# Products of 64x64 quadrants in two shared PSUM banks, in the heads stage of an RWKV-7 layer

## The chip, the cores and the metric

The kernel runs on one core of a Trainium2 chip. The metric is the device time of one execution in microseconds (us); before the change it is 1110.01 us, the median of three runs (1109.58 to 1110.29). TensorE does the matrix products, VectorE and ScalarE (DVE and ACT in the rows) the element work, GpSimd (POOL) some of it, and SyncE (SP) starts the transfers. TensorE writes its results to PSUM, which has banks of 128 partitions by 512 fp32 values.

## What is computed

A trunk of two layers on a sequence of 256 tokens with 1024 features, all in fp32. Each layer has a half-step SwiGLU FFN, a mixer and a second half-step FFN, each behind an RMS norm. The first mixer is a short gated convolution, the second is RWKV-7 time mixing with 16 heads of size 64. The change lies in the second:

```python
def wkv7_scan(r, w, k, v, a, b):          # per head: S is 64 x 64, one step per token
    def step(S, inp):
        r_t, w_t, k_t, v_t, a_t, b_t = inp
        sa = jnp.einsum('bhij,bhj->bhi', S, a_t)
        S = S * w_t[:, :, None, :] + sa[..., None] * b_t[:, :, None, :] + v_t[..., None] * k_t[:, :, None, :]
        y = jnp.einsum('bhij,bhj->bhi', S, r_t)
        return S, y
...
    y = wkv7_scan(rh, decay, kh, vh, -kk, kk * ah)
    # y is then normalised per head, gets a bonus of (r . k) v, is multiplied by the gate g
    return (y * g) @ w_o, v_first
```

## The kernel before

**Stages.** The first FFN and the convolution layer come first, then the FFN of the second layer, the inputs of the RWKV layer, its heads stage (`rwkv_heads`, L841 to L1129; 706 to 932 us of the trace) and the final FFN. Weights are streamed from HBM throughout. Large products are made of three float32r products of high and low halves (L110 to L112); the small ones of the heads stage are plain fp32 products (`mm`, L54) and transposes (`tp`, L57).

**Blocks.** The scan is done in chunks of 64 tokens. A block n is one of four groups of four heads and one half of the sequence (128 tokens, two chunks c): eight blocks in all. On a tile of 128 partitions the two halves e of the rows belong to two heads, so that a 64x64 product of a head uses one quadrant of TensorE's array, or a whole-array product uses a block-diagonal weight. Each block has four parts:

- `front(n)`: the gates and decays (`z`, `sa`, `am`, `cum`), transposes of four factors (`wT`), the scores, and the copies `bkt` (token-major factors, L940 and L941). The scores are two groups of four products of 64 rows by 128 columns (L54, into `G` for e = 0 and into the bank `G1` for e = 1). From each group `copy_predicated` (L931) puts the strictly lower part into `xfix`, and two masked products make `ar` (L936) and `br` (L938).
- `inverse(n)`, in `wkv_inverse` (L498 to L552): the inverse of four unit triangular 64x64 matrices on each row half, by doubling: levels l = 1, 2, 4, 8, 16, 32. Each level transposes the last result (L516, VectorE), copies it (`xr`, L509 or L512, ScalarE), masks the transposed one (L519 at level 1, L522 after that, VectorE) and multiplies on TensorE into the bank `xr`. At levels 2 to 16 the masked weight `pd` is 128x512: for each of four matrices a block-diagonal 128x128 weight, so four whole-array products. At levels 1 and 32 there are eight 64x64 products. Level 32 has its weights `p` from two 32-row transposes (L529) and no mask.
- `chain(n)`, in `wkv_chunk`: for the two chunks the recurrence of the state, all in the bank `ch`.
- `finish(n)`: normalisation of `y`, the gate product `g` (L991, L992) and its use (L998), transposes `oT` of the result, and its split into `oh` (ScalarE, L115) and `ol` (VectorE, L116). `g` and `oT` lie in the bank `fin`.

Projections of r, k and v for later groups and the output products (`pj`) are cut into pieces that fill TensorE between these steps.

**Order.** It is written by hand: `scores` (L1074 to L1081) has strings of letters for the steps (I an inverse step, C chain, F front, N finish, * a filler). In cycle n chain(n), inverse(n+1), finish(n−1) and front(n+2) are interleaved. VectorE and ScalarE run in the program's order (`manual_schedule`), and TensorE's products are kept in it too. Waits between engines are put in by the framework for whatever overlaps; accesses of two engines to one PSUM bank are put one after the other.

**Banks.** Eight banks: `G`, `xr`, `ch`, `fin`, two `pj` and two that are shared by the transposes and by `z`, `cum`, `G1` (`tr`). The final FFN uses the first six again (L1106, L1128).

Of the kernel before, what the change touches and what calls it, by code (L numbers as in the profile page):

```python
# [25 lines left out]
class Trunk:  # L26
# [50 lines left out]
    def bank(self, tag, name=None):  # L77
        return self.ps.tile([128, 512], F32, tag=tag, name=name or tag, bufs=self.bank_bufs[tag])
# [345 lines left out]
    def wkv_constants(self):  # L424

        nc = self.nc
# [17 lines left out]
        for l in (1, 2, 4, 8, 16):  # L444
            self.lev[l] = m = self.fixed_cols(64 if l == 1 else 128)
            nc.gpsimd.memset(m, 0.0)
            for e in range(2):
                r = slice(64 * e, 64 * e + 64)
                me = m[r] if l == 1 else m[r, 64 * e:64 * e + 64]
# [43 lines left out]
    def wkv_inverse(self, pool, u, par):  # L493
# [5 lines left out]
        src = None  # L499

        def ready(l):

            old = x0 if l == 1 else src[:, :, 1]
            xr = pool.tile([128, 4, 2, 64], F32, name=f"xr{par}", bufs=1) if l > 1 else None

            def rest():
                if l > 2:
                    n = 2 if l < 32 else 1
                    nc.scalar.copy(xr[:, :, 0:n], src[:, :, 0:n])  # L509
                elif l == 2:  # L510
                    nc.gpsimd.tensor_tensor(xr[:, :, 0], x0, all4(self.lev1T), ALU.mult)
                    nc.scalar.copy(xr[:, :, 1], src[:, :, 1])  # L512

            if l < 32:
                pb = pool.tile([128, 4, 64], F32, name=f"pb{par}", bufs=1)
                nc.vector.transpose(pb, old)  # L516
                rest()
                if l == 1:
                    nc.vector.tensor_tensor(pb, pb, all4(self.lev[l]), ALU.mult)  # L519
                else:  # L520
                    pd = pool.tile([128, 4, 2, 64], F32, name=f"pd{par}", bufs=1)
                    nc.vector.tensor_tensor(pd, pb.unsqueeze(2).broadcast_to([128, 4, 2, 64]),  # L522
                                            self.lev[l].rearrange("p (e m) -> p e m", e=2).unsqueeze(1).broadcast_to([128, 4, 2, 64]), ALU.mult)
                    pb = pd
            else:
                pb = p32
                for e in range(2):
                    lo, hi = slice(64 * e, 64 * e + 32), slice(64 * e + 32, 64 * e + 64)
                    nc.vector.transpose(pb[hi, :, 0:32], old[lo, :, 32:64])  # L529
                rest()  # L530
            return pb, xr

        pb, xr = ready(1)
        yield
        for l in (1, 2, 4, 8, 16, 32):
            i0, i1 = 0 if l > 1 else 1, 2 if l < 32 else 1
            src = self.bank("xr").rearrange("p (q i m) -> p q i m", q=4, i=2)
            for q in range(4):
                if 1 < l < 32:
                    self.mm(src[:, q], pb[:, q].rearrange("p e m -> p (e m)"), xr[:, q])  # L540
                    continue
                for e in range(2):
                    re = slice(64 * e, 64 * e + 64)
                    rhs = x0[re, q].unsqueeze(1) if l == 1 else xr[re, q, 0:i1]
                    self.mm(src[re, q, i0:i1], pb[re, q], rhs)
            yield
            if l < 32:
                pb, xr = ready(2 * l)
            else:
                u["tt"] = pool.tile([128, 2, 2, 64], F32, name="tt", bufs=2)  # L550
                nc.scalar.copy(u["tt"].rearrange("p c q m -> p (c q) m"), src[:, :, 0])
            yield  # L552
# [102 lines left out]
    def rwkv(self, normed, g, mu, wa1, prm, follow, w_gu, ctx):  # L655
        nc, tc = self.nc, self.tc
        with tc.tile_pool(name="rwkv", bufs=1, side="right", reuse_waits="tile") as cp:
# [74 lines left out]
            ctx.enter_context(self.banks(G=1, xr=1, ch=1, fin=1, pj=2))  # L732
# [108 lines left out]
    def rwkv_heads(self, pool, prm, krv, lora, gT, g2, rows, row_tile, P, loaded, follow,  # L841
# [8 lines left out]

        keep = self.tc.keep_in_program_order

        def front(n):
# [55 lines left out]
            for pair, put in (((PP, rt), lambda re, e, j: ar[re, :, :, e, j]),  # L909
                              ((b, iP), lambda re, e, j: bk[re, :, :, j ^ e])):  # L910
# [6 lines left out]
                for j in range(2):  # L917
                    for e in range(2):
                        re = slice(64 * e, 64 * e + 64)
                        nc.scalar.copy(put(re, e, j), pv[re, j])  # L920
                yield
            f = lambda z: z.rearrange("p c q t -> p (c q) t")
            by4 = lambda m, n=64: m.unsqueeze(1).broadcast_to([64, 4, n])
            for e in range(2):
                re, ro = slice(64 * e, 64 * e + 64), slice(64 - 64 * e, 128 - 64 * e)
# [6 lines left out]
                if e == 1:  # L932
                    u["inv"] = inverse(n)
                    next(u["inv"])
                    yield
# [35 lines left out]
        def finish(n):  # L971
# [17 lines left out]
            gp = self.bank("fin", "g")[:, 0:256]  # L989
# [12 lines left out]
            pt = self.bank("fin", "oT").rearrange("p (k t) -> p k t", k=4)[:, 0:2]  # L1002
# [103 lines left out]
        after.ps = [self.bank(tag, f"gu{t}") for t, tag in enumerate(("G", "xr"))]  # L1106
# [21 lines left out]
        self.mm_tags = deque(("ch", "fin", "pj", "pj", "G", "xr"))  # L1128
# [78 lines left out]
```

## Time and profile before

| | before |
|---|---|
| median of three runs | 1110.01 us (1109.58 to 1110.29) |
| profiled execution | 1109.84 us, of which the span is 1108.1 |
| TensorE busy in the span | 98% |
| VectorE, ScalarE, GpSimd busy | 64%, 51%, 10% |
| chain that ended last, by engine | TensorE 70%, issue 18%, VectorE 8%, ScalarE 2% |
| heads stage | 706 to 932 us |

The busy shares are means over stages with different limits: outside the heads stage TensorE multiplies large weights all the time. Matmuls are pipelined, so the time from the start of one group to the start of the next tells what a group costs; the time of a single record is longer than its share.

### The profile page before, as it was taken

How to read it: one execution, taken by the hardware profiler on the slowest of the kernel's cores; microseconds unless marked ns; L12 is line 12 of the kernel's file. 1: busy time of each engine (PE TensorE's matmuls, PEld its weight loads, DVE VectorE, ACT ScalarE, POOL GpSimd, SP SyncE). 2: the span in 40 equal slices, each digit the busy share in tenths (PEclk: the TensorE clock that was granted, in tenths of full speed). 3: DMA queues.
4: the chain of work that ended last, by engine and by line, in shares of the span. 5: the costliest groups of instructions: out<-in, count | busy, mean ns of one | idle time of the engine just before them, and what ended most of it. 6: DMA issues, size and time to landing. Idle time of an engine off the chain costs nothing.

```text
span 1108.1 us, 15866 instructions
## 1 busy us (share of the span) xinstructions
PE 1081.7 (98%) x6064; PEld 897.4 (81%) x6064; DVE 711.0 (64%) x1021; ACT 562.8 (51%) x893; POOL 113.0 (10%) x201
## 2 busy tenths in 40 slices
PE   7999999999999999999999999999999999999997
PEld 5888888788878888878888778988887767888886
DVE  5656644787676655476664547568999986555535
ACT  7555543655565544365554334446766536444433
POOL 6000000000410000000000001223434220000000
PEclk9999999999999999999999999999999999999999
DMA  8998887698599986769989825753342737566551
GB/s 286 310 295 271 283 262 258 208 357 269 174 335 333 295 291 222 253 210 349 320 272 354 304 76 169 280 194 128 113 126 98 252 96 231 174 183 201 186 190 38
DMA packets 164340, 256.19 MB, mean 231 GB/s; under 512 B 10414, under 2 KB 128934, under 8 KB 164264
## 3 DMA queue, kind: packets, MB, share of 16 engines
q1 hardware_dynamic: 164264, 255.17, 69.3%
q8 instruction: 48, 0.79, 0.3%
q14 instruction: 28, 0.23, 0.1%
HBM read 216.34 MB, written 38.80 MB: 230 GB/s over the span
## 4 chain that ended last, share of the span: by engine, by line
PE 70%; issue 18%; DVE 8%; ACT 2%; DMA 0%; SPq 0%; POOL 0%; POOLq 0%; ACTq 0%; DVEq 0%
PE gu L111 11%; PE gu L112 11%; PE gu L110 11%; PE acc L112 6%; PE acc L111 6%; PE acc L110 6%; PE ci L111 2%; PE ci L112 2%; PE ci L110 2%; PE pj L110 2%; PE xr L54 2%; PE pj L112 1%; PE pj L111 1%; PE aT L351 1%; PE ch L54 1%
## 5 line engine op out<-in xcount | busy, mean ns | idle before, releaser
L111 PE MATMUL gu<-lo_gu,xh 128*128 128x512 f32 x688 | 272.2, 396 | 2.8 <-DVE lo_gu L105 2.7
L112 PE MATMUL gu<-hi_gu,xl 128*128 128x512 f32 x688 | 271.9, 395 | 0.0
L110 PE MATMUL gu<-hi_gu,xh 128*128 128x512 f32 x688 | 268.9, 393 | 0.7 <-ACT xh L176 0.7
L105 DVE TENSOR_TENSOR lo_gu<-raw_gu,hi_gu 128x2048 fp32r<-128x2048 f32 (+2 forms) x92 | 198.4, 2159 | 107.7 <-ACT hi_gu L104 105.4
L105 DVE TENSOR_TENSOR lo_o<-raw_o,hi_o 128x2048 fp32r<-128x2048 f32 x48 | 109.4, 2291 | 114.8 <-ACT hi_o L104 114.7
L104 ACT CAST hi_gu<-raw_gu 128x2048 fp32r<-128x2048 f32 (+2 forms) x92 | 164.9, 1796 | 30.6 <-DMA raw_gu<-in_ffn_w_gu_dram 13.7
L111 PEld LDWEIGHTS gu<-lo_gu,xh 128*128 128x128 f32 x688 | 129.6, 188 | 30.3 <-DVE lo_gu L105 4.8
L110 PEld LDWEIGHTS gu<-hi_gu,xh 128*128 128x128 f32 x688 | 129.5, 188 | 26.7 <-ACT xh L176 1.1
L112 PEld LDWEIGHTS gu<-hi_gu,xl 128*128 128x128 f32 x688 | 129.6, 188 | 25.0 <-DVE xl L178 0.4
L104 ACT CAST hi_o<-raw_o 128x2048 fp32r<-128x2048 f32 x48 | 90.9, 1909 | 100.8 <-PE acc L112 95.9
L111 PE MATMUL acc<-lo_o,ah 128*128 128x512 f32 (+1 forms) x356 | 138.0, 388 | 2.2 <-DVE lo_o L105 2.2
L112 PE MATMUL acc<-hi_o,al 128*128 128x512 f32 (+1 forms) x356 | 137.8, 388 | 0.0
L110 PE MATMUL acc<-hi_o,ah 128*128 128x512 f32 (+1 forms) x356 | 131.1, 388 | 0.0
L345 ACT ACTIVATE s<-gu,rs 128x256 f32<-128x256 f32 x88 | 41.7, 475 | 111.7 <-PE gu L112 111.6
L148 POOL TENSOR_TENSOR rs<-ms,fixed 128x1 f32<-128x1 f32 x14 | 8.9, 639 | 821.4 <-DVE ms L146 821.3
L111 PEld LDWEIGHTS acc<-lo_o,ah 128*128 128x128 f32 x356 | 66.9, 188 | 16.4 <-DVE lo_o L105 3.1
L112 PEld LDWEIGHTS acc<-hi_o,al 128*128 128x128 f32 x356 | 66.9, 188 | 13.4
L110 PEld LDWEIGHTS acc<-hi_o,ah 128*128 128x128 f32 x356 | 66.7, 188 | 13.3
L115 ACT CAST ah<-aT 128x512 fp32r<-128x512 f32 x44 | 25.8, 586 | 87.8 <-PE aT L351 87.8
L349 DVE SCALAR_TENSOR_TENSOR a<-gu,rs,s 128x256 f32<-128x256 f32 x88 | 41.9, 480 | 42.9 <-ACT s L345 42.7
L616 ACT CAST hl_p<-hl_p 128x512 fp32r<-128x512 f32 x72 | 44.3, 624 | 29.5 <-DMA hl_p<-in_rwkv_w_rkv_dram 19.7
L116 DVE TENSOR_TENSOR al<-aT,ah 128x512 fp32r<-128x512 f32 x44 | 30.3, 690 | 35.1 <-ACT ah L115 35.1
(263 smaller groups left out, 1638.7 us busy)
## 6 DMA issues: line engine op xcount, KB each, us to landing
raw_gu<-in_ffn_w_gu_dram SPq DMA_DIRECT2D x164, 512.0 KB, 5.5
raw_o<-in_ffn_w_d_dram SPq DMA_DIRECT2D x44, 1024.0 KB, 5.7
parts<-hl_p SPq DMA_DIRECT2D x72, 512.0 KB, 7.1
hl_n<-parts SPq DMA_DIRECT2D x52, 512.0 KB, 4.0
hl_p<-in_rwkv_w_rkv_dram SPq DMA_DIRECT2D x48, 256.0 KB, 7.4
raw_ci<-in_conv_w_in_dram SPq DMA_DIRECT2D x14, 512.0 KB, 7.1
raw_ci<-in_conv_w_in_dram SPq DMA_DIRECT2D x4, 1024.0 KB, 9.3
raw_o<-in_conv_w_out_dram SPq DMA_DIRECT2D x4, 1024.0 KB, 8.8
```

Of the source, the lines that this page charges most:

```text
L54: self.tc.keep_in_program_order(self.nc.tensor.matmul(out, lhsT, rhs, start=True, stop=True))
L104: nc.scalar.copy(hi[:, ks], raw[:, ks])
L105: nc.vector.tensor_tensor(lo[:, ks], raw[:, ks], hi[:, ks].bitcast(F32), ALU.subtract)
L110: keep(mm(out, xh, wh, start=start, stop=False))
L111: keep(mm(out, xh, wl, start=False, stop=False))
L112: keep(mm(out, xl, wh, start=False, stop=stop))
L115: keep(self.nc.scalar.copy(hi, src))
L116: keep(self.nc.vector.tensor_tensor(lo, src, hi.bitcast(F32), ALU.subtract))
L345: act = nc.scalar.activation(s, ps[t][:, 0:256], AF.Silu, scale=rstd[t])
L349: nc.vector.scalar_tensor_tensor(a, ps[t][:, 256:512], rstd[t], s, ALU.mult, ALU.mult)
L351: nc.tensor.transpose(out=pt[:, j, t * 128:t * 128 + 128], in_=a[:, j * 128:(j + 1) * 128], identity=self.ident)
L616: nc.scalar.copy(hi, lo)
```

## The change

The four level products of 128x128 at levels 2 to 16 become eight products of a 64x64 weight with a 64x128 operand. Chunk c = 0 stays on the diagonal quadrants (row half e to column half e), chunk c = 1 goes to the crossed ones (`to = e ^ c`) and into a second bank, so the masks have 64 columns and the mask product is 128x256 in place (`pb`, no `pd`). The result's columns have a new order (chunk, matrix, ...), which the rearrangements follow.

The scores become one group of 16 products of 64x64 weights: those of each half with its own rows into `G` (diagonal), the others crossed into `G1`. One `copy_predicated` and one `br` product on 128 rows take the place of two each on 64; the inverse is started straight behind the `copy_predicated`; the two `ar` products stay, and behind them come all eight `bkt` copies.

The banks `xr` and `fin` become one tile of two banks, `pair`. The inverse uses columns 256:512 of both, `g` and `oT` columns 0:256 of the first. In the final FFN the same two banks go by `pair0` and `pair1`.

```diff
     def bank(self, tag, name=None):
+        if tag in ("pair0", "pair1"):
+            return self.pair[:, int(tag[-1])]
         return self.ps.tile([128, 512], F32, tag=tag, name=name or tag, bufs=self.bank_bufs[tag])
...
-                    pd = pool.tile([128, 4, 2, 64], F32, name=f"pd{par}", bufs=1)
-                    nc.vector.tensor_tensor(pd, pb.unsqueeze(2).broadcast_to([128, 4, 2, 64]),
...
-                    pb = pd
+                nc.vector.tensor_tensor(pb, pb, all4(self.lev[l]), ALU.mult)
...
-            for q in range(4):
-                if 1 < l < 32:
-                    self.mm(src[:, q], pb[:, q].rearrange("p e m -> p (e m)"), xr[:, q])
-                    continue
...
+            for q in range(2):
+                for c in range(2):
+                    for e in range(2):
+
+                        to = e ^ (c if 1 < l < 32 else 0)
+                        re, out = slice(64 * e, 64 * e + 64), slice(64 * to, 64 * to + 64)
+                        i = 2 * c + q
+                        rhs = x0[re, i].unsqueeze(1) if l == 1 else xr[re, i, 0:i1]
+                        self.mm(src[out, c, q, i0:i1], pb[re, i], rhs)
...
-                g = (self.tr_bank("G1") if e else self.bank("G")).rearrange("p (c q s t) -> p c q s t", c=2, q=2, s=2)
-                for c in range(2):
-                    for p in range(2):
-                        self.mm(g[:, c, p], bk[re, c, p], ar[re, c, p, e])
-                yield
-                nc.vector.copy_predicated(x0[re], by4(self.strict[re]).bitcast(mybir.dt.uint32), f(g[re, :, :, 0]))
...
+            for c in range(2):
+                for p in range(2):
+                    for e, re, ro in own:
+                        self.mm(gb[re, c, p], bk[re, c, p, 0], ar[re, c, p, e])
+                    for e, re, ro in own:
+                        self.mm(gk[ro, c, p], bk[re, c, p, 1], ar[re, c, p, e])
+            yield
+            nc.vector.copy_predicated(x0, by4(self.strict).bitcast(mybir.dt.uint32), f(gb[:, :, :, 0]))
+            u["inv"] = inverse(n)
+            next(u["inv"])
+            yield
+            nc.vector.tensor_tensor(f(br), f(gb[:, :, :, 1]), by4(self.incl), ALU.mult)
+            yield
+            for e, re, ro in own:
                 nc.vector.tensor_tensor(ar[ro, :, :, e].rearrange("p c q s t -> p (c q) (s t)"),
...
-            for i, _ in enumerate(self.wkv_inverse(pool, us[n], n % 2)):
+            for i, _ in enumerate(self.wkv_inverse(pool, us[n], n % 2, duo[:, :, 256:512])):
...
-            gp = self.bank("fin", "g")[:, 0:256]
+            gp = duo[:, 0, 0:256]
...
-            pt = self.bank("fin", "oT").rearrange("p (k t) -> p k t", k=4)[:, 0:2]
+            pt = duo[:, 0, 0:256].rearrange("p (k t) -> p k t", k=2)
...
-        self.mm_tags = deque(("ch", "fin", "pj", "pj", "G", "xr"))
+        self.mm_tags = deque(("ch", "pair0", "pj", "pj", "G", "pair1"))
```

How instructions stand on two engines in one steady cycle, before and after; lines of the changed program have other numbers. **First place:** ScalarE from the end of level 16 to the split of the output. `xr` with 128x4x64 is the copy ahead of level 32, `bkt` are the eight token-major copies of the block in `front`, `oh` is the first half of the split in `finish`. Before:

```order
L940 COPY bkt<-b 64x2x64
L941 COPY bkt<-iP 64x2x64
L940 COPY bkt<-b 64x2x64
L941 COPY bkt<-iP 64x2x64
L509 COPY xr_7687<-xr 128x4x64
L580 COPY hvu<-ch 64x2x64
L582 COPY y<-ch 64x2x64 x2
L940 COPY bkt<-b 64x2x64
L941 COPY bkt<-iP 64x2x64
L940 COPY bkt<-b 64x2x64
L941 COPY bkt<-iP 64x2x64
L115 CAST oh<-oT 128x2x128
```

After:

```order
L513 COPY xr_7746<-pair 128x4x64
L578 COPY hvu<-ch 64x2x64
L580 COPY y<-ch 64x2x64 x2
L948 COPY bkt<-b 64x2x64
L949 COPY bkt<-iP 64x2x64
L948 COPY bkt<-b 64x2x64
L949 COPY bkt<-iP 64x2x64
L948 COPY bkt<-b 64x2x64
L949 COPY bkt<-iP 64x2x64
L948 COPY bkt<-b 64x2x64
L949 COPY bkt<-iP 64x2x64
L117 CAST oh<-pair 128x2x128
```

Four `bkt` copies moved from ahead of the `xr` copy to behind it; `oh` has eight ahead of it there instead of four.

**Second place:** TensorE at level 32 with what each instruction waits for (the engine's semaphore). `PT` are transposes in `front`, `xr<-..,p` (after: `pair<-..,p`) is level 32, `ch` are products of the chain, `z` those of the next block's gates. Before:

```order
L57 MATMUL PT<-fixed,P 128x128 [waits DVE_49,PE_49]
L57 MATMUL PT<-fixed,P 128x128
L54 MATMUL xr<-xr_7050,p_5671 64x64 [waits Activation_49]
L54 MATMUL xr<-xr_7050,p_5671 64x64 x7
L54 MATMUL ch<-hvu,bkt 64x64 [waits DVE_49,Activation_49]
L54 MATMUL ch<-hvu,bkt 64x64 x3
L54 MATMUL ch<-hvu,br 64x64 x4
L54 MATMUL z<-w_5292,wT 128x256
L54 MATMUL z<-a_5294,aT 128x256
```

After:

```order
L57 MATMUL PT<-fixed,P 128x128 [waits PE_49]
L57 MATMUL PT<-fixed,P 128x128
L54 MATMUL pair<-xr_7093,p_5671 64x64 [waits DVE_49]
L54 MATMUL pair<-xr_7093,p_5671 64x64 x7
L54 MATMUL ch<-hvu,bkt 64x64 [waits Activation_49]
L54 MATMUL ch<-hvu,bkt 64x64 x3
L54 MATMUL ch<-hvu,br 64x64 x4
L54 MATMUL z<-w_5292,wT 128x256
L54 MATMUL z<-a_5294,aT 128x256
```

The products stand in the same order; the first of level 32 waits for VectorE instead of ScalarE.

**Third place:** VectorE around the transposes into `p` (L529, after: L527). `xfix` is the copy of the scores into the next inverse, `pb<-xfix` and `pb<-pb` its first transpose and mask. Before:

```order
L931 COPY_PREDICATED xfix_5666<-fixed,G 64x256
L936 TENSOR_TENSOR ar<-G,fixed 64x4x128
L938 TENSOR_TENSOR br<-G,fixed 64x256
L529 STREAM_TRANSPOSE p_5671<-xr 32x4x32 x2
L580 COPY hvu<-ch 64x2x64
L931 COPY_PREDICATED xfix_5666<-fixed,G_7682 64x256
L516 STREAM_TRANSPOSE pb_7699<-xfix_5666 128x256
L519 TENSOR_TENSOR pb_7699<-pb_7699,fixed 128x256
L936 TENSOR_TENSOR ar<-G_7682,fixed 64x4x128
L938 TENSOR_TENSOR br<-G_7682,fixed 64x256
L116 TENSOR_TENSOR ol<-oT,oh 128x2x128
```

After:

```order
L1006 TENSOR_TENSOR y<-y,pair 128x256
L938 COPY_PREDICATED xfix_5666<-fixed,G 128x256
L520 STREAM_TRANSPOSE pb_7742<-xfix_5666 128x256
L522 TENSOR_TENSOR pb_7742<-pb_7742,fixed 128x256
L942 TENSOR_TENSOR br<-G,fixed 128x256
L527 STREAM_TRANSPOSE p_5671<-pair 32x4x32 x2
```

The first transpose and mask of the next inverse moved ahead of the transposes into `p`; both `ar` products moved behind them, still ahead of `ol`.

## Rows read from the trace of the kernel before

**Rows 1.** The page's first part: busy us, share and instructions of each engine.

```profile
PE 1081.7 (98%) x6064; PEld 897.4 (81%) x6064; DVE 711.0 (64%) x1021; ACT 562.8 (51%) x893; POOL 113.0 (10%) x201
```

**Rows 2.** Windows: length, busy us and count per engine, PEclk, DMA share, GB/s.

```profile
706.00:728.00 22.00, 21.96 (x167) 20.84 (x166) 11.08 (x26) 11.76 (x29) 5.20 (x7) 1.00 0.65 198
728.00:767.00 39.00, 38.15 (x386) 33.73 (x386) 30.18 (x68) 25.51 (x74) 11.43 (x17) 1.00 0.42 144
...
820.00:840.00 20.00, 18.49 (x194) 15.37 (x191) 19.00 (x47) 12.82 (x41) 7.04 (x10) 1.00 0.38 109
```

**Rows 3.** Chain of waits from 800 to 860 us, its shares by line.

```profile
by line: DVE pd L522 11.5%; DVE pb L516 6.4%; issue 6.3%; DVE hvu L595 4.8%; DVE y L599 4.5%; DVE ar L936 4.0%; DVE br L938 3.5%; DVE p L529 3.1%; DVE kk L889 2.9%; DVE xfix L931 2.7%; ACT xr L509 2.4%; DVE am L874 2.4%; DVE b L895 2.3%; DV
```

**Rows 4.** TensorE's timeline: start us, us, engine line op out<-in xcount; level 16, scores.

```profile
846.38 1.16 PE L54 MATMUL xr<-xr,pd 128*128 128x128 f32 x8
847.47 1.16 PE L54 MATMUL G<-ar,bk 64*128 64x128 f32 x8
848.55 0.44 PE L57 MATMUL oT<-fixed,y 128*128 128x128 f32 x2
```

**Rows 5.** TensorE's timeline, level 32 and the chain's crossed products.

```profile
829.39 0.51 PE L54 MATMUL xr<-xr,p 64*64 64x64 f32 x10
829.69 0.27 PE L54 MATMUL ch<-hvu,br 64*64 64x64 f32 x2
...
830.07 0.70 PE L54 MATMUL z<-w,wT 65*128 65x256 f32 x2
```

**Rows 6.** VectorE's groups, 706 to 932: count, busy us, mean ns, idle before.

```profile
L522 DVE TENSOR_TENSOR pd<-pb,fixed 128x512 f32<-128x512 f32 x32 | 25.3, 791 | 1.1
...
L931 DVE COPY_PREDICATED xfix<-fixed,G 64x256 f32<-64x256 uint32 x16 | 7.1, 443 | 7.4 <-PE G L54 7.1
...
L938 DVE TENSOR_TENSOR br<-G,fixed 64x256 f32<-64x256 f32 x16 | 6.7, 422 | 0.2
...
L519 DVE TENSOR_TENSOR pb<-pb,fixed 128x256 f32<-128x256 f32 x8 | 4.8, 605 | 0.3
```

**Rows 7.** ScalarE's timeline, second half of a head group.

```profile
850.31 0.30 ACT L940 COPY bkt<-b 64x128 f32<-64x128 f32 x1
...
851.25 0.30 ACT L941 COPY bkt<-iP 64x128 f32<-64x128 f32 x1
851.45 0.36 ACT L115 CAST oh<-oT 128x256 fp32r<-128x256 f32 x1
...
852.40 0.60 ACT L868 ACTIVATE sa<-z 128x512 f32<-128x512 f32 x1 [0.26 <-PE z L54]
```

**Rows 8.** VectorE's timeline of the same stretch: transposes into p, split, next cycle.

```profile
848.45 0.64 DVE L529 STREAM_TRANSPOSE p<-xr 32x128 f32<-32x128 f32 x2
...
852.21 0.42 DVE L116 TENSOR_TENSOR ol<-oT,oh 128x256 fp32r<-128x256 f32 x1
...
854.78 0.43 DVE L873 SCALAR_TENSOR_TENSOR am<-sa,rows 128x256 f32<-128x256 f32 x1
```

**Rows 9.** TensorE's timeline of the same stretch, from level 32.

```profile
849.86 0.68 PE L54 MATMUL xr<-xr,p 64*64 64x64 f32 x16
850.47 0.45 PE L54 MATMUL ch<-hvu,bkt 128*64 128x64 f32 x8
850.85 0.45 PE L54 MATMUL ch<-hvu,br 64*64 64x64 f32 x8
851.23 0.70 PE L54 MATMUL z<-w,wT 65*128 65x256 f32 x2
```

**Rows 10.** Timelines of VectorE and ScalarE, first half of a head group.

```profile
827.21 0.64 DVE L529 STREAM_TRANSPOSE p<-xr 32x128 f32<-32x128 f32 x2
...
832.67 0.43 DVE L873 SCALAR_TENSOR_TENSOR am<-sa,rows 128x256 f32<-128x256 f32 x1
...
830.21 0.57 ACT L704 COPY pr<-pj 128x512 f32<-128x512 f32 x1
...
831.27 0.60 ACT L868 ACTIVATE sa<-z 128x512 f32<-128x512 f32 x1
```

More of the change, by code (lines that the diff above doesn't have):

```diff
@@ L444, in wkv_constants @@
         for l in (1, 2, 4, 8, 16):
-            self.lev[l] = m = self.fixed_cols(64 if l == 1 else 128)
+            self.lev[l] = m = self.fixed_cols(64)
             nc.gpsimd.memset(m, 0.0)
@@ L448, in wkv_constants @@
                 r = slice(64 * e, 64 * e + 64)
-                me = m[r] if l == 1 else m[r, 64 * e:64 * e + 64]
+                me = m[r]
                 v = me.rearrange("p (b h r) -> p b h r", h=2, r=l)[:, :, 0]
@@ L498, in wkv_inverse @@
         all4 = lambda m: m.unsqueeze(1).broadcast_to([128, 4, 64])
-        src = None
+        by2 = lambda z: z.rearrange("p (c q) m -> p c q m", c=2)
+        src = duo.rearrange("p c (q i m) -> p c q i m", q=2, i=2)
         def ready(l):
-            old = x0 if l == 1 else src[:, :, 1]
+            old = by2(x0) if l == 1 else src[:, :, :, 1]
             xr = pool.tile([128, 4, 2, 64], F32, name=f"xr{par}", bufs=1) if l > 1 else None
@@ L528, in ready @@
                     lo, hi = slice(64 * e, 64 * e + 32), slice(64 * e + 32, 64 * e + 64)
-                    nc.vector.transpose(pb[hi, :, 0:32], old[lo, :, 32:64])
+                    nc.vector.transpose(by2(pb)[hi, :, :, 0:32], old[lo, :, :, 32:64])
                 rest()
@@ L550, in wkv_inverse @@
                 u["tt"] = pool.tile([128, 2, 2, 64], F32, name="tt", bufs=2)
-                nc.scalar.copy(u["tt"].rearrange("p c q m -> p (c q) m"), src[:, :, 0])
+                nc.scalar.copy(u["tt"], src[:, :, :, 0])
             yield
@@ L730, in first_weights @@
                             yield ("gu", 4 * kh + k, u), [z[:, k:k + 2, u] for z in parts]
-            ctx.enter_context(self.banks(G=1, xr=1, ch=1, fin=1, pj=2))
+            ctx.enter_context(self.banks(G=1, ch=1, pj=2))
+            self.pair = self.ps.tile([128, 2, 512], F32, name="pair", bufs=1)
             with tc.tile_pool(name="rwkvB", bufs=1, reuse_waits="tile") as pool:
@@ L849, in rwkv_heads @@
         us, o = [], {}
+        duo = self.pair
         keep = self.tc.keep_in_program_order
@@ L907, in front @@
             bk = pool.tile([128, 2, 2, 2, 64], F32, name="bk")
-            for pair, put in (((PP, rt), lambda re, e, j: ar[re, :, :, e, j]),
-                              ((b, iP), lambda re, e, j: bk[re, :, :, j ^ e])):
+            for pair, own in (((PP, rt), True), ((b, iP), False)):
                 pt = self.tr_bank("wT").rearrange("p (i q t) -> p i q t", i=2, q=2)
@@ L917, in front @@
                 for j in range(2):
-                    for e in range(2):
-                        re = slice(64 * e, 64 * e + 64)
-                        nc.scalar.copy(put(re, e, j), pv[re, j])
+                    if own:
+                        for e in range(2):
+                            re = slice(64 * e, 64 * e + 64)
+                            nc.scalar.copy(ar[re, :, :, e, j], pv[re, j])
+                    else:
+                        nc.scalar.copy(bk[:, :, :, j], pv[:, j])
@@ L921, in front @@
                 yield
             f = lambda z: z.rearrange("p c q t -> p (c q) t")
-            by4 = lambda m, n=64: m.unsqueeze(1).broadcast_to([64, 4, n])
-            for e in range(2):
-                re, ro = slice(64 * e, 64 * e + 64), slice(64 - 64 * e, 128 - 64 * e)
-                g = (self.tr_bank("G1") if e else self.bank("G")).rearrange("p (c q s t) -> p c q s t", c=2, q=2, s=2)
-                for c in range(2):
-                    for p in range(2):
-                        self.mm(g[:, c, p], bk[re, c, p], ar[re, c, p, e])
-                yield
-                nc.vector.copy_predicated(x0[re], by4(self.strict[re]).bitcast(mybir.dt.uint32), f(g[re, :, :, 0]))
[L932 to L935, printed above, removed]
+            by4 = lambda m, n=64: m.unsqueeze(1).broadcast_to([m.shape[0], 4, n])
@@ new lines, in front @@
+            gb, gk = (z.rearrange("p (c q s t) -> p c q s t", c=2, q=2, s=2)
+                      for z in (self.bank("G"), self.tr_bank("G1")))
+            own = [(e, slice(64 * e, 64 * e + 64), slice(64 - 64 * e, 128 - 64 * e)) for e in range(2)]
+            for c in range(2):
[4 more added lines that the diff above has]
+                        self.mm(gk[ro, c, p], bk[re, c, p, 1], ar[re, c, p, e])
@@ L938, in front @@
-                nc.vector.tensor_tensor(f(br[re]), f(g[re, :, :, 1]), by4(self.incl[re]), ALU.mult)
+                                        gk[ro].rearrange("p c q s t -> p (c q) (s t)"), by4(self.masks[ro], 128), ALU.mult)
                 for c in range(2):
@@ L1104, in rwkv_heads @@
                     row_tile(n // 2, "ln_w", "ln_b")
-        after.ps = [self.bank(tag, f"gu{t}") for t, tag in enumerate(("G", "xr"))]
+        after.ps = [self.bank(tag, f"gu{t}") for t, tag in enumerate(("G", "pair1"))]
         def inner(t, k):
```

18 lines of the change are left out of this document (4 added, 14 removed).

## The prediction

> **What bounds the kernel now.** I read the page first, then windows of the stage that the change touches, then its chain of waits, then single stretches. TensorE is busy for 98% of the span [rows 1], and the clock is granted in full in the windows of the stage [rows 2]. So the first thought is that any TensorE time saved comes off the total. The windows of the heads stage (706 to 932 us) correct that: from 706 to 728 TensorE is full and VectorE half empty, but from 820 to 840 VectorE is at 19.0 of 20 us and TensorE has 1.5 us of holes. The chain of waits there [rows 3] runs over VectorE: the masked weights of the inverse (L522) lead with 11.5%, then the transposes (L516). The stage is a ring: scores, inverse, chain, finish of different blocks hand work around TensorE, VectorE and ScalarE, in an order written out by hand. A step counts only if it is on the ring.
>
> **Part 1, the level products.** A level's group (eight records; each fp32 matmul leaves two) takes 1.09 us: 846.38 to the next group at 847.47 [rows 4]. A group of 16 quadrant records with 64 columns takes 0.61 (849.86 to 850.47) [rows 9]; two row halves go side by side, so that is eight steps of 0.058 and 0.15 of edges. With 128 columns a step is 0.115. If four quadrants run at once, a level is 4 × 0.115 + 0.15 = 0.61 and saves 0.48; if only two, 8 × 0.115 + 0.15 = 1.07 and saves 0.02. Rows that bear on it: at 829.69 a crossed group (`br`) starts inside the diagonal one (`xr`), and both are over at 830.07, 0.68 after 829.39 [rows 5]; one after the other they take 0.61 and 0.38 (850.85 to 851.23) [rows 9]. Four at once is what this shows, so I take 0.48. Four levels in eight blocks: 15 us of TensorE.
>
> The 0.15 of edges is what a quadrant group loses between whole-array neighbours. The Trainium skill ("TensorEngine Tiling (Array Packing)", Key Properties) says that a change of tiling mode drains the array, which speaks against turning 32 whole-array groups into quadrant groups. Without a drain a level would save 0.63, 5 us more in all; the row has the edge, so 0.48 stands.
>
> **Part 2, the scores.** Before, two groups of eight records, 1.08 each (847.47 to 848.55 [rows 4]), 2.16 in all. After, 32 records: 8 × 0.115 + 0.15 = 1.07 with four quadrants at once (saves 1.1), 1.99 with two (saves 0.2). Eight blocks: 9 us. TensorE saves 24 us in all.
>
> **Part 3, VectorE and ScalarE.** L522 falls from 128x512 (791 ns) to 128x256 in place; the nearest row, the same product at level 1, has 605 (L519), a plain 128x256 product about 420 [rows 6]. So 0.19 to 0.37 each, four per block. One `copy_predicated` on 128 rows replaces two on 64 (443 ns): −0.44; the same for `br`: −0.42. In all 1.6 to 2.3 us per block, 13 to 19 in eight. On ScalarE four copies of 64 rows become two of 128; it is not the bound there. The masks change only constants that are built hundreds of us earlier, at nothing.
>
> **Part 4, the waits that are added.** `fin` and `xr` become one pair of banks. The order [second place] shows the level-32 product waiting for VectorE where it waited for ScalarE. By the semaphore counts of the built program that VectorE instruction is `ol`, the second half of the split of the previous block's transposed output (L116, after L118): it reads columns 0:256 of the bank into which level 32 writes. `ol` waits for the cast `oh` on ScalarE, and there the order [first place] shows a second thing: four of the eight `bkt` copies, which ran ahead of the `xr` copy before level 32, now stand behind it, and all eight ahead of `oh`. Queued behind level 32 on TensorE are the chain's `bkt` and `br` products and the next block's `z`; for `z` waits `sa` on ScalarE, and for `sa` waits `am` on VectorE, the head of the next cycle.
>
> The Trainium skill ("PSUM — Partial Sum Buffer", the section on bank collisions) has two engines kept apart per bank and 32-partition quadrant, disjoint columns included. By that rule the wait stays although the columns differ; were it by columns, level 32 would go as before and the time would be that of rival 1. No run so far shows which; the built order has the wait.
>
> Its price, from the end T of the transposes into `p` (T = 849.09: 848.45 + 0.64 [rows 8]). The first `bkt` copy now in that place starts at 850.31, T + 1.22, and their step is (851.25 − 850.31)/3 = 0.31 [rows 7]. Eight: `oh` starts at T + 3.73, takes 0.36 [rows 7], `ol` 0.42 [rows 8]: level 32 at T + 4.55, where it was T + 0.77 (849.86) [rows 9]. From level 32 to `sa` is 2.54 (852.40), `sa` takes 0.60 [rows 7]: `am` at T + 7.7. Before, it was at 854.78, T + 5.7 [rows 8]; VectorE has nothing else to do in between than what it had. **+2.0** for a cycle of this kind (second half of a head group). In the other kind T = 827.85, `sa` comes 1.88 after level 32 (829.39 to 831.27) and `am` at 832.67, T + 4.8 [rows 5, 10]; after: 4.55 + 1.88 + 0.60 = T + 7.0, **+2.2**, and +0.5 more in the one cycle where a copy of `pr` (830.21) stands ahead of `oh` [rows 10].
>
> Five cycles have a finish beside an inverse that is followed by a front (blocks 1 to 5): 2.2 + 2.0 + 2.7 + 2.0 + 2.2 = **+11.1**.
>
> **What is won against it.** Between `am` and the next T, part 3 saves four times 0.19 to 0.37, 0.7 to 1.5 us per cycle. (`copy_predicated` and `br` change nothing there: as much VectorE work still comes ahead of the transposes into `p`, since the next inverse's first transpose and mask are pulled forward.) Against it stands another new wait: level 16 now waits for `y*g` on VectorE (L998), which stands behind the mask of that level, two products of 0.42, some 0.85 us. I take −0.5 per cycle, with ends of −1.5 and 0: **−2.5**.
>
> Ahead of 767 us no finish runs beside an inverse, so there the change only saves. Up to there TensorE loses three score groups and eight levels, 7.2 us, and it is nearly full (38.15 of 39) [rows 2]. But an inverse goes product, copy, transpose, mask, product, and part of the shortened products only lengthens the wait for the next mask. I take block 0's scores (1.1), block 1's levels (1.9) and 0.8 of the rest: **−3.8**; ends −1.1 and −7.2.
>
> After block 6 and in the final FFN only the banks' names change: 0, give or take 1.
>
> **Sum.** 11.1 − 2.5 − 3.8 = +4.8. The profiled execution took 1109.84 (span 1108.1 and 1.7 around it), the median of the runs 1110.01, so nothing needs adjusting: 1109.9 + 4.8 = **1114.7**. With the ends of both gains (0 to −7.5, −1.1 to −7.2): 1106 to 1120.
>
> **Rivals.** 1. *Faster: the new wait is no loss, the stage goes by VectorE's own work.* For it: VectorE is full from 820 to 840, and 1.6 us per block is taken off it; TensorE has 24 us less to do and could fill the holes. It decides for this if `oh` is out within about 2.5 us of T instead of 3.7, or if level 32 is late anyway because of the filler products ahead of it. Then 8 × 1.6 = 13 comes off: **1097**, 1091 at the far end. Against it: level 32 follows the fillers ahead of it at T + 0.8 and T + 1.5 in the rows [rows 5, 9], and eight copies are 2.5 us whatever else happens.
> 2. *The quadrants don't do what they say: two run at a time.* The gain up to 767 shrinks to some −0.8, and the levels save nothing later: **1118**. Against it stand rows 5; their groups, though, have 64 columns a record and not 128, and overlap only for some 0.3 us.
> 3. *Balance.* The middle gain is at its upper end and the early one too: 11.1 − 7.5 − 5 lies near zero, **1109 to 1112**.
> 4. *The clock.* TensorE gets two holes of over 2 us per cycle. In the window with 1.5 us of holes in 20 it is still granted 1.00 [rows 2]. If the lower level of 1.2 GHz followed each of the ten holes for as long as the hole, ten times 1.2 us would be added: **1126**. Nothing in the rows speaks for it.
>
> **Chances.** Forecast 0.48 (own range 1109 to 1119), rival 1 with cases on the way to it 0.22, rival 2 0.11, rival 3 0.14, rival 4 0.05. The predicted time is the forecast's. Leaving out the lower half of rival 1 and rival 4 gives the range 1101 to 1121. A measurement here can tell 0.2% (2.2 us) from nothing: faster, below 1107.8: rival 1 and a little of the forecast's lower tail, 0.25. Same: rival 3 and the lower part of the forecast, 0.20. Slower: the rest, 0.55.
>
> **What would show it.** Right: VectorE has a hole of about 2 us ahead of `ol` in five cycles, TensorE one ahead of level 32 of the same size and a second ahead of the next cycle's first products; level groups 0.6 us apart and a score group about 1.1; `am` of block 1 earlier than before by some 4 us and that of block 4 later by 3. Wrong: level 32 starts within 2.5 us of T, or `am` to `am` in the steady cycles is shorter than before (then rival 1); level groups of 1.05 (rival 2); a granted clock below 1.00 between 767 and 900 (rival 4). The step I trust least is what a cycle wins between `am` and T.

## The result and the profile after

The changed kernel takes 1123.98 us (median of four, 1119.54 to 1125.15) against 1109.8: a ratio of 1.012, interval 1.0092 to 1.0148. The forecast had the sign; the size was 4.8 us and came out as 14.2, beyond the range's upper end of 1121.

| | before | after |
|---|---|---|
| profiled execution, span | 1109.84, 1108.1 us | 1125.15, 1123.4 us |
| TensorE busy | 1081.7 us (98%) | 1071.4 us (95%) |
| VectorE busy | 711.0 us | 692.7 us |
| TensorE at its lower clock, 728 to 930 us | 0 us | 34 us |

The page's first part after the change, which answers to [rows 1]: TensorE is busy for 10 us less and VectorE for 18, in a longer span.

```profile
PE 1071.4 (95%) x6448; PEld 881.0 (78%) x6448; DVE 692.7 (62%) x1005; ACT 555.9 (49%) x877; POOL 111.3 (10%) x201
```

Windows of the changed kernel (length, busy us and count of TensorE, its weight loads, VectorE, ScalarE, GpSimd; then TensorE's granted clock, the share of the DMA engines, GB/s), which answer to [rows 2]:

```profile
728.00:767.00 39.00, 36.30 (x516) 30.32 (x511) 29.65 (x75) 25.47 (x75) 12.51 (x19) 1.00 0.45 150
...
800.00:820.00 20.00, 15.17 (x181) 12.83 (x180) 12.55 (x34) 8.84 (x27) 4.07 (x8) 0.74 0.21 66
820.00:840.00 20.00, 16.33 (x232) 13.56 (x224) 14.25 (x39) 11.78 (x36) 5.62 (x7) 0.91 0.43 127
...
860.00:880.00 20.00, 18.47 (x210) 14.41 (x210) 14.37 (x41) 8.76 (x25) 6.62 (x9) 0.83 0.60 192
```

The kernel before, same columns:

```profile
800.00:820.00 20.00, 20.00 (x228) 17.93 (x226) 19.00 (x47) 12.50 (x38) 6.85 (x11) 1.00 0.38 126
```

Up to 767 us the stage is freer than before and the clock is full. From 800 on neither TensorE nor VectorE is full any more: 15.2 and 12.6 of 20 us, where they had 20.0 and 19.0. Each waits for the other. And there is a column that was 1.00 in every window of 2 us from 728 to 930 before: the clock, 0.74 from 800 to 820.

**The wait is where the prediction put it.** VectorE and ScalarE of the first steady cycle (timeline: start us, us, engine, line, operation, out<-in, count, and in brackets the idle time before it and who ended it):

```profile
778.47 0.64 DVE L527 STREAM_TRANSPOSE p<-pair 32x128 f32<-32x128 f32 x2
...
779.45 1.39 DVE L945 TENSOR_TENSOR ar<-G,fixed 64x512 f32<-64x512 f32 x2
783.09 0.42 DVE L118 TENSOR_TENSOR ol<-pair,oh 128x256 fp32r<-128x256 f32 x1 [2.25 <-ACT oh L117]
...
786.27 0.42 DVE L874 SCALAR_TENSOR_TENSOR am<-sa,rows 128x256 f32<-128x256 f32 x1 [1.28 <-ACT sa L869]
```

```profile
779.21 0.37 ACT L513 COPY xr<-pair 128x256 f32<-128x256 f32 x1 [2.39 <-DVE p L527]
...
780.33 0.30 ACT L948 COPY bkt<-b 64x128 f32<-64x128 f32 x1
...
782.50 0.30 ACT L949 COPY bkt<-iP 64x128 f32<-64x128 f32 x1
782.70 0.36 ACT L117 CAST oh<-pair 128x256 fp32r<-128x256 f32 x1
```

T, the end of the transposes into `p`, is 778.47 + 0.64 = 779.11. `oh` starts at T + 3.6, behind eight `bkt` copies 0.31 apart, and VectorE stands idle for 2.25 us until it can do `ol`. In the cycles 1 to 5 level 32 starts 4.46, 4.47, 4.95, 4.47 and 4.51 us after T; forecast were 4.55, and 5.0 in the one with the `pr` copy. `am` of a cycle is here the one behind its level 32, which ends the cycle: that of cycle 1 is at 786.27, 7.2 after T (forecast 7.0).

**What was not priced.** TensorE in the second steady cycle, same columns:

```profile
804.59 0.44 PE L57 MATMUL pair<-fixed,y 128*128 128x128 f32 x2 [2.30 <-ACT xr L513]
...
808.53 1.12 PE L54 MATMUL pair<-xr,p 64*64 64x64 f32 x16 [2.26 <-DVE ol L118]
809.58 0.69 PE L54 MATMUL ch<-hvu,bkt 128*64 128x64 f32 x8
...
810.82 1.22 PE L54 MATMUL z<-w,wT 65*128 65x256 f32 x2
811.83 1.06 PE L54 MATMUL z<-a,aT 65*128 65x256 f32 x2
```

Two holes of 2.3 us follow each other. The second is the known one, for `ol`. The first stands ahead of the transposes `oT` (`pair<-fixed,y`), which wait for ScalarE's `xr` copy of the level-32 input, again because they write into the bank that it reads; the prediction had not listed this wait. The second hole that it did list, ahead of the next cycle's first products, is not there: once level 32 has run, TensorE is full for 4 us and more. Then the groups themselves are slow: level 32 takes 1.05 us to the next group (808.53 to 809.58) where [rows 9] have 0.61, and `z` goes on at 811.83, 1.01 after 810.82. TensorE works at 1.2 GHz there, and its products from level 32 to `am` are on the ring: 5.03 us from level 32 to `am`, forecast 3.14.

How the clock goes around the first such place, in windows of 2 us:

```profile
780.00:782.00 2.00, 1.73 (x15) 1.49 (x13) 0.82 (x2) 1.91 (x8) 0.00 (x0) 1.00 0.00 0
782.00:784.00 2.00, 0.43 (x18) 0.43 (x22) 0.87 (x3) 1.08 (x5) 0.00 (x0) 1.00 0.72 231
784.00:786.00 2.00, 2.00 (x25) 1.76 (x18) 0.62 (x3) 0.73 (x2) 0.00 (x0) 0.75 0.11 39
786.00:788.00 2.00, 2.00 (x11) 1.87 (x9) 1.35 (x4) 0.65 (x2) 0.24 (x1) 0.50 0.01 4
788.00:790.00 2.00, 2.00 (x25) 1.69 (x24) 0.87 (x2) 0.96 (x2) 0.78 (x1) 0.89 0.38 102
```

After a stretch with 0.43 us of products in 2 us the granted clock falls from 1.00 to 0.50, stays there while TensorE is full again, and is back some 3 us later. In cycles 2 and 4 it stays down for some 10 us. Added up over the windows of 2 us from 728 to 930, 0.50 being the lower level, that is 34 us at 1.2 GHz.

The quadrants do what the change says. A level and a score group in stretches at full clock:

```profile
729.41 0.67 PE L54 MATMUL pair<-xr,pb 64*64 64x128 f32 x16
730.01 0.39 PE L112 MATMUL pj<-hl_n,xvh 128*128 128x256 f32 x1
```

```profile
775.31 1.10 PE L54 MATMUL G<-ar,bk 64*64 64x128 f32 x32
776.24 0.40 PE L54 MATMUL ch<-rc,tt 64*64 64x64 f32 x8
```

A level takes 0.60 to the next group and the scores 0.93, against 1.09 and 2.16 [rows 4]; forecast were 0.61 and 1.07.

### The profile page after: what moved, and what is told of

Same layout as the page of the kernel before. It is cut to its first block, busy times and chain, and to the rows that moved or that the text cites. A ratio compares the mean times of both kernels' runs of the same rounds, so it can differ in the third digit from the quotient of the medians.

```text
span 1123.4 us, 16585 instructions
## 1 busy us (share of the span) xinstructions
PE 1071.4 (95%) x6448; PEld 881.0 (78%) x6448; DVE 692.7 (62%) x1005; ACT 555.9 (49%) x877; POOL 111.3 (10%) x201
## 4 chain that ended last, share of the span: by engine, by line
PE 70%; issue 18%; DVE 6%; ACT 4%; DMA 1%; SPq 0%; POOL 0%; POOLq 0%; ACTq 0%; DVEq 0%
PE gu L113 9%; PE gu L114 9%; PE gu L112 9%; PE acc L114 6%; PE acc L113 6%; PE acc L112 6%; PE pj L112 2%; PE ci L113 2%; PE ci L114 2%; PE ci L112 2%; PE pair L54 2%; PE pair L114 2%; PE pair L112 2%; PE pair L113 2%; PE pj L113 2%
## 5 line engine op out<-in xcount | busy, mean ns | idle before, releaser
L113 PE MATMUL gu<-lo_gu,xh 128*128 128x512 f32 x632 | 249.7, 395 | 3.1 <-DVE lo_gu L107 3.1
L114 PE MATMUL gu<-hi_gu,xl 128*128 128x512 f32 x632 | 249.7, 395 | 0.0
L112 PE MATMUL gu<-hi_gu,xh 128*128 128x512 f32 x632 | 247.0, 394 | 1.6 <-ACT xh L178 0.9
L113 PEld LDWEIGHTS gu<-lo_gu,xh 128*128 128x128 f32 x632 | 118.9, 188 | 28.6 <-DVE lo_gu L107 5.0
L112 PEld LDWEIGHTS gu<-hi_gu,xh 128*128 128x128 f32 x632 | 118.8, 188 | 25.7 <-ACT xh L178 1.3
L114 PEld LDWEIGHTS gu<-hi_gu,xl 128*128 128x128 f32 x632 | 119.0, 188 | 23.3 <-DVE xl L180 0.4
L113 PE MATMUL acc<-lo_o,ah 128*128 128x512 f32 (+1 forms) x334 | 129.6, 389 | 2.3 <-DVE lo_o L107 2.3
L114 PE MATMUL acc<-hi_o,al 128*128 128x512 f32 (+1 forms) x334 | 129.5, 389 | 0.0
L112 PE MATMUL acc<-hi_o,ah 128*128 128x512 f32 (+1 forms) x334 | 123.1, 390 | 0.0
L615 DVE TENSOR_TENSOR hl_p<-hl_p 128x512 fp32r<-128x512 f32 x72 | 48.0, 684 | 4.6 <-ACT hl_p L614 4.6
```

What stands on the lines that cost most here:

```text
L112: keep(mm(out, xh, wh, start=start, stop=False))
L113: keep(mm(out, xh, wl, start=False, stop=False))
L114: keep(mm(out, xl, wh, start=False, stop=stop))
L615: nc.vector.tensor_tensor(lo.bitcast(F32R), lo, hi.bitcast(F32), ALU.subtract)
```

## Experiments

Theory from here on: level 32 and `oT`, and for a little while level 16, wait because `g` and `oT` share the inverse's bank; `oh` is late because of the `bkt` copies; and the holes that this leaves in TensorE lower its clock, which makes a loss of some 5 us one of 14. Rivals: the quadrant products cost by themselves; the clock does no harm; the clock is all.

### g and oT out of the inverse's bank

```diff
-            gp = duo[:, 0, 0:256]
+            gp = self.tr_bank("g")[:, 0:256]
...
-            pt = duo[:, 0, 0:256].rearrange("p (k t) -> p k t", k=2)
+            pt = self.tr_bank("oT")[:, 0:256].rearrange("p (k t) -> p k t", k=2)
```

> The changed kernel, but g and oT go into the two rotating transpose banks; the inverse shares its banks with nothing. Order of all instructions as in the changed kernel. Theory (level 32 is late because it waits for ol, and the holes lower the clock): level 32 is back at T + 0.8 to 1.5 (T: end of the transposes into p), VectorE still idles some 2 us ahead of ol because oh stands behind eight bkt copies, am at T + 5.7 to 6.9; clock 1.00 or close; time 1104 to 1110, that is, no slower than the kernel before. Rival (the quadrant products or their banks themselves are what costs): 1120 to 1124 as now. Rival (the clock alone, whatever waits): clock as now, 1115 to 1124.

Measured: 1106.03 us, ratio 0.9959 (0.9945 to 0.9974), faster than before the change. Two lines take 18 us off. Level 32 of the first steady cycle, and VectorE there:

```profile
783.35 0.68 PE L54 MATMUL pair<-xr,p 64*64 64x64 f32 x16 [0.65 <-ACT xr L513]
```

```profile
782.18 0.64 DVE L527 STREAM_TRANSPOSE p<-pair 32x128 f32<-32x128 f32 x2
...
786.80 0.42 DVE L118 TENSOR_TENSOR ol<-oT,oh 128x256 fp32r<-128x256 f32 x1 [2.25 <-ACT oh L117]
...
788.39 0.43 DVE L874 SCALAR_TENSOR_TENSOR am<-sa,rows 128x256 f32<-128x256 f32 x1
```

T is 782.82. Level 32 follows at T + 0.53 and waits for its `xr` copy alone. `ol` still waits 2.25 us for `oh`, as expected, and `am` is at T + 5.6. So the shared bank is the cause of the wait, and the quadrant products are not what costs. The clock is not clean yet: 17 us at the lower level in the trace, an execution of 1110.70 us. Over the six executions of this one program the time goes with the clock: 1110.70 us at a mean granted clock of 0.990, 1104.17 at 0.999.

### The bkt copies ahead of the xr copy

`tok(e)` is the loop of four `bkt` copies of row half e, taken out of the last step of the scores:

```diff
...
             u["inv"] = inverse(n)
             next(u["inv"])
+            tok(0)
             yield
             nc.vector.tensor_tensor(f(br), f(gb[:, :, :, 1]), by4(self.incl), ALU.mult)
+            tok(1)
...
```

> The changed kernel with its shared banks, but all eight bkt copies stand ahead of the xr copy of level 32 on ScalarE, four behind copy_predicated and four behind br. Theory: the wait for ol stays but is short; oh at T + 1.3, level 32 at T + 2.1, am at T + 4.6 to 5.2; clock back at 1.00; 1099 to 1105. Rival (sharing the bank costs by itself, wherever oh stands, since level 16 and oT wait too): 1110 to 1118. Rival (the quadrant products cost): 1120 to 1124.

Measured: 1115.92, ratio 1.0057 (1.0039 to 1.0074). 8 us better than the change, but 11 above the theory's upper end; the first rival's number. ScalarE and TensorE of the first steady cycle:

```profile
778.61 0.37 ACT L513 COPY xr<-pair 128x256 f32<-128x256 f32 x1 [0.40 <-DVE p L527]
...
779.76 0.37 ACT L117 CAST oh<-pair 128x256 fp32r<-128x256 f32 x1
```

```profile
779.04 0.69 PE L57 MATMUL pair<-fixed,y 128*128 128x128 f32 x2 [2.24 <-ACT xr L513]
779.38 0.56 PE L112 MATMUL pj<-hl_n,xvh 128*128 128x256 f32 x1
...
782.09 0.63 PE L57 MATMUL PT<-fixed,P 128*128 128x128 f32 x2
782.64 0.80 PE L54 MATMUL pair<-xr,p 64*64 64x64 f32 x10
```

T is 778.51. `oh` is early, at T + 1.25, as meant. But level 32 comes at T + 4.1: `oT` had to wait for the `xr` copy (2.24 us of hole), twelve filler products stand between `oT` and level 32, and they now run at the lower clock, 0.21 us apart instead of 0.12. The third wait of the shared bank, hidden behind the wait for `ol` until then, has become the last one in this cycle. The cycles differ: level 32 comes 4.1, 2.2, 5.2, 2.9 and 3.3 us after T, and in the third and fifth it waits for `ol` again; in the third `oh` stands behind the `pr` copy, which waits for slow fillers. And 34 us are at the lower clock, as many as with the change itself. My expectation had let `oT` go on as before.

### Both

> Both: g and oT in the transpose banks and the eight bkt copies ahead of the xr copy. Theory: no wait of level 32 for ol and no wait of ol for copies; per cycle 1.6 to 2.3 us of VectorE are saved: 1092 to 1099. Rival (quadrant products cost, or TensorE's saving is hidden anyway): 1107 to 1112 or slower.

Measured: 1100.16 (1097.28 to 1104.63), ratio 0.9916 (0.9891 to 0.9942). In the expected direction, one us short. The four kernels side by side:

| median us | bkt behind the xr copy | bkt ahead |
|---|---|---|
| g and oT in the inverse's bank | 1124.0 (the change) | 1115.9 |
| g and oT elsewhere | 1106.0 | 1100.2 |

The bank is worth 16 to 18 us, the place of the copies 6 to 8.

### The hole ahead of level 32 filled

The waits stay; ten extra products, whose result nobody uses, run in TensorE's hole.

```diff
...
+            if 3 <= n <= 7:
+                for i in range(10):
+                    self.mm(whole[:, 256:384], self.cum, P[:, 0:128])
```

> The changed kernel with its wait, but ten extra products of 128x128 (some 0.2 us each; results are not used) between PT and level 32 in cycles 1 to 5, which fill the hole there and nothing else. If the lowered clock is what made 14 us out of the 5 that the waits give: clock 1.00 or nearly through the stage and 1113 to 1118 in spite of more work. If the clock is harmless and the waits are all: 1122 to 1127, as now or a bit slower. If the hole ahead of oT (behind level 16) is enough to lower the clock: clock still below 1.00 in the stage, 1120 to 1125.

Measured: 1120.96 (1119.17 to 1125.06), ratio 1.0105 (1.0084 to 1.0126). That is the third of the expectations: the hole ahead of `oT` is enough to lower the clock. In the trace (1119.17 us) the clock is at 1.00 up to 820 us and `am` of cycle 2 at 810.30 instead of 813.56, but it falls in later windows (0.87 from 830 to 840), where the hole ahead of `oT` is still open.

### Both holes filled

On top of the products of the last run:

```diff
+            if n < 6:
+                warm = self.tr_bank("warm")
+                for j in range(10):
+                    self.mm(warm[:, 0:128], self.cum, self.ident)
             for j in range(2):
                 self.tp(pt[:, j], y[:, j * 128:(j + 1) * 128])
```

> The changed kernel as in the run with one hole filled, and ten more extra products (results not used) between level 16 and oT, where TensorE has its other hole of 2.2 us. Theory (the clock makes the rest of the loss): clock 1.00 from 767 to 900, am of the cycles 1 to 4 at 763, 786, 811, 835 and 858 within 1 us, and 1113 to 1117, in spite of some 45 us more products. Rival (what is left of the loss is waits, and the products come on top): 1120 to 1127.

Measured: 1117.4 (1116.68 to 1118.52), ratio 1.0066 (1.0051 to 1.0081): 6.6 us faster than the change with more work on TensorE, and 0.4 above the range expected. Windows and one start of `am`:

```profile
800.00:820.00 20.00, 19.68 (x247) 17.66 (x240) 14.84 (x41) 10.77 (x33) 6.59 (x9) 1.00 0.40 123
820.00:840.00 20.00, 19.32 (x264) 16.53 (x262) 15.06 (x42) 10.69 (x33) 5.08 (x7) 1.00 0.34 97
```

```profile
857.83 0.43 DVE L874 SCALAR_TENSOR_TENSOR am<-sa,rows 128x256 f32<-128x256 f32 x1
```

The clock is 1.00 in every window of 2 us from 728 to 930, so it is not the quadrant products themselves that lower it. With the clock kept, the waits give what was worked out from the rows of before: `am` of the cycles 1 to 4 at 785.68, 809.89, 834.28 and 857.83 (expected 786, 811, 835, 858). The next run had the products ahead of `oT` only up to cycle 4:

> The changed kernel with both holes filled by extra products (results not used), those ahead of oT only up to cycle 4: in cycle 5 of the run with two holes filled there was no hole ahead of oT, and the products pushed oT and, through the copy of PT, oh by 2 us. If waits alone make the forecast's time once the clock is kept: 1114.5 to 1116.5, clock 1.00 from 767 to 880. If the 1117.4 of that run was not those 2 us: 1117 to 1119.

Measured: 1116.62 (1115.05 to 1118.05), ratio 1.0059 (1.0044 to 1.0074), with 3 us at the lower clock: between the two ranges expected. This run and the last overlap, so what separates them from 1114.7 isn't settled by this: about 2 us, with the extra products' own cost among them.

### Holes filled where no wait is left

The kernel with both repairs, with four extra products between `PT` and level 32 from block 2 on:

> The kernel with g and oT in the transpose banks and bkt ahead, with four extra products of 128x128 between PT and level 32 (results not used), where TensorE has 0.65 us of hole. If its clock of 0.993 costs it something and the hole is what lowers it: clock 1.00 and 1095 to 1099. If the freed TensorE time lowers the clock elsewhere all the same: clock as it was and 1100 to 1103.

Measured: 1096.09 (1095.15 to 1096.36), ratio 0.9874 (0.9857 to 0.989), the fastest of all. Windows of the kernel with both repairs, without and then with the extra products:

```profile
796.00:798.00 2.00, 1.19 (x10) 0.94 (x8) 1.89 (x6) 1.91 (x8) 0.74 (x1) 1.00 0.10 16
798.00:800.00 2.00, 1.32 (x28) 0.95 (x28) 1.92 (x5) 1.78 (x8) 0.00 (x0) 0.98 0.65 246
800.00:802.00 2.00, 2.00 (x12) 1.61 (x13) 1.92 (x9) 0.21 (x1) 0.00 (x0) 0.50 0.03 8
...
806.00:808.00 2.00, 2.00 (x21) 1.55 (x20) 1.03 (x3) 0.37 (x1) 0.00 (x0) 0.82 0.83 278
```

```profile
796.00:798.00 2.00, 1.54 (x24) 1.12 (x16) 1.93 (x5) 1.92 (x8) 0.73 (x1) 1.00 0.03 8
798.00:800.00 2.00, 1.68 (x24) 1.59 (x26) 1.88 (x6) 1.78 (x7) 0.00 (x0) 1.00 0.66 219
800.00:802.00 2.00, 2.00 (x30) 1.69 (x26) 1.94 (x7) 0.75 (x4) 0.00 (x0) 1.00 0.11 43
```

Without them TensorE is busy for 1.19 and 1.32 of 2 us, in holes of 0.81 us and less, and the clock falls for 7 us; in all 13.6 us are at the lower level. With them it stays at 1.00 throughout. The control puts the same products into the kernel before:

> The kernel before with four extra products of 128x128 between PT and level 32 in each block from cycle 0 on (results not used), as in the run that reached 1096. TensorE is full there, so they come on top: some 6 times 0.45 to 0.9 us, 1112 to 1116. If extra products gained time by themselves: under 1109.5.

Measured: 1112.2 (1111.58 to 1114.13), ratio 1.0022 (1.0012 to 1.0031). They cost 2 us there, where the clock was full anyway. So what they gain in the repaired kernel is put down to the clock; no other way for idle products to gain shows in these runs.

### Both chunks in diagonal quadrants

The kernel with both repairs, with `to = e` at every level:

```diff
-                        to = e ^ (c if 1 < l < 32 else 0)
+                        to = e
```

> The same kernel with both chunks of levels 2 to 16 in diagonal quadrants (the two banks stay): two quadrants at a time and not four. If four run at once in the crossed form: a level group goes from 0.6 to 1.07 us and the total from 1100 to 1103 to 1110 (up to 1.9 us per cycle on the ring). If the crossing brings nothing: group and total as they were, 1098 to 1102.

Measured: 1101.41 (1101.04 to 1101.78), ratio 0.9921 (0.9906 to 0.9936). The group, at the same place as above:

```profile
728.25 1.09 PE L54 MATMUL pair<-xr,pb 64*64 64x128 f32 x16
729.27 0.39 PE L112 MATMUL pj<-hl_n,xvh 128*128 128x256 f32 x1
```

The group went as the first theory has it, the total as the second. 1.02 to the next group instead of 0.60, so four quadrants do run at once in the crossed form and two in this one. Yet the total hardly moves (1100.16 with a wide spread against 1101.41): the diagonal form keeps TensorE busier and has 3.4 us at the lower clock where the crossed one has 13.6. What the crossing saves is given back by the clock: at `am` of cycle 1 the crossed kernel is 2.2 us ahead (781.77 against 783.95), and at that of cycle 3, behind its 7 us at the lower level, 0.4 (826.11 against 826.53). Against the run with filled holes, 1096.09, the crossing shows; the diagonal form with filled holes was not run.

### Each half alone

The kernel before with the new scores only, its own banks and `bkt` ahead of the `xr` copy; and with the new levels only, `g` and `oT` in the transpose banks:

> The kernel before with its whole-array levels and its own banks xr and fin; only the scores are as in the change, with the eight bkt copies ahead of the xr copy. Theory: no new wait; VectorE saves 0.86 us per block and TensorE 1.1: 1101 to 1106. Rival (the scores' new order of steps costs by itself): 1109 to 1115.

> The levels in crossed quadrants of two banks with masks of 64 columns, g and oT in the transpose banks; scores and bkt as in the kernel before. VectorE saves 0.74 us per block by its rows and TensorE 1.9. If the stage goes by VectorE: 6 us less, 1103 to 1106. If TensorE's saving counts as well: 1098 to 1102. If the clock falls with the freed TensorE time: 1105 to 1110.

Measured: the scores alone 1101.98 (1101.77 to 1102.24), ratio 0.9926 (0.9911 to 0.9941), with no time at the lower clock; the levels alone 1105.92 (1103.8 to 1106.48), ratio 0.996 (0.9945 to 0.9974), with 7 us at it. Each is faster than before without the shared bank. The levels' second result lies at the border of two expectations and doesn't part them.

## Why the prediction was wrong

- **Right: the wait and its price.** Level 32 behind `ol`, `ol` behind `oh`, `oh` behind eight copies: 4.46 to 4.95 us after T in five cycles, as forecast (the terms for 4.55 add up to 4.51). With the clock kept (both holes filled), T to `am` takes 2.59, 1.97, 2.60 and 1.98 us longer than before in the cycles 1 to 4; forecast were 2.2, 2.0, 2.7 and 2.0. By the sum, the `am` ahead of the first of these waits comes 3.8 earlier than before and the one behind the fourth 3.1 later (the prediction's "block 1" and "block 4", which do not count alike). Measured in that run are 4.9 earlier and 3.05 later (857.83 against 854.78). Before, and with both holes filled:

```profile
767.05 0.43 DVE L873 SCALAR_TENSOR_TENSOR am<-sa,rows 128x256 f32<-128x256 f32 x1
```

```profile
762.15 0.42 DVE L874 SCALAR_TENSOR_TENSOR am<-sa,rows 128x256 f32<-128x256 f32 x1 [0.66 <-ACT sa L869]
```

- **Luck in the sum.** The gain up to 767 us was taken 1.1 too small and that of the cycles too large: `am` to the next T is shorter by 0.50, 0.29 and 0.54 and once longer by 0.14, where 0.5 was taken off each. These two errors nearly cancel. The masks' own saving was within its bounds: 517 ns a product, where the prediction had 605 and about 420 (the latter read from a line of 64 rows in [rows 6]).

```profile
L522 DVE TENSOR_TENSOR pb<-pb,fixed 128x256 f32<-128x256 f32 x40 | 20.7, 517 | 1.4
```

- **Wrong: the clock, rival 4.** The sum has every group at the full clock and gives the loss of clock nothing; the rival got 0.05, with the sentence "Nothing in the rows speaks for it". The step that failed is reading a clock of 1.00 in a window with 1.5 us of holes in 20 as a sign that two holes of 2.3 us, some 2 us apart, would do no harm. What the runs showed in its place is 34 us at 1.2 GHz, in five stretches of 3 to 10 us. The rival's price, 1126, was near by luck: it had ten stretches as long as their holes. A row of the kernel before that I had not looked at speaks for it: at the end, when TensorE runs out of work,

```profile
1090.00:1100.00 10.00, 10.00 (x50) 8.44 (x49) 5.47 (x11) 2.30 (x6) 0.55 (x1) 1.00 0.01 2
1100.00:1108.00 8.00, 1.98 (x17) 1.78 (x15) 3.23 (x9) 2.34 (x7) 0.55 (x1) 0.76 0.35 131
```

  the clock is below 1.00 with 1.98 us of products in 8. Of the 14.2 us, 6.6 to 7.4 go when the clock is kept by filling the holes (1117.4 and 1116.6), some 5 are the forecast's waits less gains, and about 2 stay open, the extra products' own cost among them.
- **Missed: the third wait of the shared bank**, `oT` behind the `xr` copy. It was not late itself, being covered by the wait for `ol`, so the sum needed no term for it; but it made the first of the two holes, and it is what the run with early `bkt` copies ran into.
- **Right: four quadrants at once**, and what a group costs: 0.60 against the 0.61 worked out, and 1.02 with two at a time against 1.07. The Trainium skill ("TensorEngine Tiling (Array Packing)", Key Properties) has the array drained at a change of tiling mode. The groups cost no more than was worked out from [rows 9] with its edge; whether that edge is a drain, no run here shows. The scores were over-priced by 0.14 (0.93 against 1.07).
- **The bank rule.** The Trainium skill ("PSUM — Partial Sum Buffer", bank collisions) keeps two engines out of one bank and quadrant whatever the columns; the kernel's own waits follow it, and moving `g` and `oT` took them away (level 32 at T + 0.53 instead of T + 4.46). What the chip would do without the wait was not tried.
- **The gain was there.** Rival 1 had 1097 for a stage without the waits. The repaired kernels reach 1100.2, and 1096.1 once the clock is kept.

## To carry to other kernels

In a program whose waits go by the bank, as here, two tiles that share a PSUM bank share its waits, whichever columns they use: list every pair of engines that touches the bank and price each wait by what is queued behind it, in the order the changed program really has. Work taken off a full TensorE leaves holes, and here the holes lowered its clock: count the gain only after reading the granted clock in windows of 2 us around each hole. A hole that can't be avoided may be cheaper filled with work that nobody needs than left empty, which a control run on the unchanged kernel must show.

## What the hardware showed unexpectedly

The granted clock fell after holes of 0.81 us and less when several stood close together: in the kernel with both repairs at 800 us, after 1.19 and 1.32 us of products in two windows of 2 us, to 0.50 for about 7 us. The Trainium skill ("TensorE: Matmul & The Clock Gate", A second HAM failure mode) tells of a clock that swings when TensorE idles briefly and often between groups; this trace agrees, with 13.6 us at the lower level. Filling the holes took some 4 us off the time (1100.16 against 1096.09). And in the changed kernel the clock, once down, stayed down while TensorE was full again, for some 3 us in one cycle and 10 in others, so that the holes slowed products that had nothing to do with it.
